# Dilated 3x3 convolution: an eight-row store on four DMA engines, moved from the last image pair to the first

## The chip, the cores and the metric

One core of one Trainium2 chip. The metric is the device time of one execution in microseconds. The figure for the kernel before is the median of six runs.

## The reference

The input x has 16 images of 64 channels, 64 x 64 pixels, in float32. The weights have 128 output channels, 64 input channels and 3 x 3 taps. The dilation is 2, so the input is padded by 2 on each side and the output has the same 64 x 64 pixels:

```python
for b, co, ci, kh, kw in ...:
    output[b, co] += weight[co, ci, kh, kw] * x_pad[b, ci, kh*2:kh*2+64, kw*2:kw*2+64]
```

The input is 16.8 MB, the output 33.6 MB, and each is moved once.

## The kernel before, in words

**Tiling.** Two images make a pair: their 2 x 64 input channels fill the 128 partitions, and a row of the partition is one channel of one image, 64 x 64 pixels. There are eight pairs (`npairs`). A pair is worked through in four groups (`NG`) of 16 output rows (`GR`), so the main loop over `G` (line 193) has 32 turns, with `pb` the pair and `g` the group in it.

**A turn.** ScalarE casts chunks of a pair's float32 tile `x32` to float16, several groups ahead (`casts`, line 153, which calls `cast`, line 68). VectorE adds pairs of rows (`rowsum`, line 77). TensorE makes three products in PSUM: psP from the row sums, psA and psB from the rows themselves (`product`, line 161); output rows come in blocks of four, of which two are psA + psP and two are psB + psP. ScalarE copies psP to SBUF (line 227), and VectorE does the two additions (line 234), which write the group's 16 rows of both images into the pair's output tile `osb`. That tile has 128 partitions, one for each output channel, and in each partition the first image's 64 rows and then the second's.

**Buffers.** `x32`, `x16` and `osb` have three buffers each. A load into an `x32` buffer waits until the casts of the pair three earlier have read it, and the additions into an `osb` buffer wait until the stores of the pair three earlier have landed.

**The order of the DMAs.** All loads and stores are issued from SyncE (SP) into one queue, in the order in which the program is written; SP stands still when an issue has to wait. The schedule is written by hand. Ahead of the loop come the weights (line 88), the first pair in two parts and the second and the third pair whole (lines 89 to 91; `load`, line 61, with the issue at line 64). The fourth pair's load is issued at the end of turn `G == 0` (lines 241 and 242), the fifth pair's at the end of the first pair (lines 253 and 254), later ones at the ends of pairs (line 243). A DMA also waits, eight DMAs later, for the one whose semaphore it takes over.

**Stores.** `store` (line 183) writes rows r0 to r1 of image m of a pair; its last argument cuts the 128 partitions into several DMAs, by default one. The middle pairs are stored at their end, 2 MB for each image (lines 255 to 257). The first and the last pair are stored in halves, after the second and the fourth group (lines 245 to 252), 1 MB for each image. One of these halves is cut further: for the second image of the last pair, rows 0 to 23 go out as one DMA (line 249) and rows 24 to 31 as two (line 250): 124 partitions (`FOUR`, line 190), and then the remaining 4, with 2 KB in each partition. `ROWS4` (line 191) is 8. The profile shows these two DMAs on four of the sixteen DMA engines.

**The end.** At line 290 SP waits for all stores to land, one semaphore after another.

Of the kernel before, what the change touches and what calls it, by code (L numbers as in the profile page):

```python
# [10 lines left out]
def kernel(  # L11
# [24 lines left out]
    GR = 16  # L36
# [24 lines left out]
    def load(pb, cuts=(0, H)):  # L61
        x32_tiles[pb] = fpool.tile([P, HW], f32, tag="x32", name="x32")
        for lo, hi in zip(cuts[:-1], cuts[1:]):
            nc.sync.dma_start(  # L64
                out=x32_tiles[pb][:, lo * W : hi * W], in_=x_pair[pb, :, lo * W : hi * W]
            )
# [10 lines left out]
    def rowsum(c):  # L77
        pb, g = divmod(c, NG)
        if g == 0:
            xs_tiles[pb] = sxpool.tile([P, HW // 2], f16, tag="xs", name="xs")  # L80
        v = x16_tiles[pb][:, g * GR * W : (g + 1) * GR * W].rearrange(
            "p (b e q) -> p b e q", e=2, q=2 * W
        )
        s = xs_tiles[pb][:, g * NH : (g + 1) * NH].rearrange("p (b q) -> p b q", q=2 * W)
        nc.vector.tensor_tensor(out=s, in0=v[:, :, 0], in1=v[:, :, 1], op=add)  # L85
# [67 lines left out]
    def casts(G):  # L153
        for n in range(2 if G else 3):
            c = ahead[0]
            if c >= ngroups or c > G + (7 if c < 2 * NG else 5):
                return
            cast(c)
            ahead[0] += 1

    def product(ps, src, kind, blk0, nblk, first, last):
        for j in (1, 0, 2):
            dw = (j - 1) * d
            o0, o1 = max(0, -dw), W - max(0, dw)
            t = kind * KW + j
            for hb in range(2):
                pp = slice(hb * CI, (hb + 1) * CI)
                rhs = src(pp, dw + o0, dw + o1)
                po = ps[:, hb * NH + blk0 * 2 * W : hb * NH + (blk0 + nblk) * 2 * W]
                po = po.rearrange("p (r w) -> p r w", w=W)[:, :, o0:o1]  # L170
                nc.tensor.matmul(  # L171
                    out=po,
                    lhsT=w_sb[pp, t * CO : (t + 1) * CO],
                    rhs=rhs,
                    start=first and j == 1,
                    stop=last and j == 2,
                )

    def blocks(x16, b0, n, e):
        v = x16.rearrange("p (b e r w) -> p b e r w", e=2, r=2, w=W)  # L180
        return lambda pp, c0, c1: v[pp, b0 : b0 + n, e, :, c0:c1]

    def store(pb, m, r0=0, r1=H, rows=((0, P),)):
        for lo, hi in rows:
            nc.sync.dma_start(
                out=out_img[2 * pb + m, lo:hi, r0 * W : r1 * W],
                in_=o_tiles[pb][lo:hi, m * HW + r0 * W : m * HW + r1 * W],
            )

    FOUR = ((0, P - 4), (P - 4, P))  # L190
    ROWS4 = 8

    for G in range(ngroups):
        pb, g = divmod(G, NG)
        x16 = x16_tiles[pb]
        xs = xs_tiles[pb].rearrange("p (r w) -> p r w", w=W)
        if g == 0:
            o_tiles[pb] = opool.tile([P, 2 * HW], f32, tag="osb", name="osb")
        o = o_tiles[pb].rearrange("p (m b e q) -> p m b e q", m=2, e=2, q=2 * W)
        b0 = g * NBLK  # L200

        def summed():
            ps = ppool.tile([P, 2 * NH], f32, tag="p", name="psP")
            sv = lambda pp, c0, c1: xs[pp, g * GR // 2 : (g + 1) * GR // 2, c0:c1]
            product(ps, sv, 0, 0, NBLK, True, True)
            return ps

        if G:
            psP = summed()

        psA = apool.tile([P, 2 * NH], f32, tag="ab", name="psA")
        product(psA, blocks(x16, b0, NBLK, 1), 1, 0, NBLK, True, False)
        z = 1 if g == 0 else 0
        product(psA, blocks(x16, b0 + z - 1, NBLK - z, 1), 2, z, NBLK - z, False, True)

        psB = apool.tile([P, 2 * NH], f32, tag="ab", name="psB")
        product(psB, blocks(x16, b0, NBLK, 0), 3, 0, NBLK, True, False)
        z = 1 if g == NG - 1 else 0
        product(psB, blocks(x16, b0 + 1, NBLK - z, 0), 4, 0, NBLK - z, False, True)

        if not G:
            psP = summed()

        if not G:
            casts(0)
        p_sb = spool.tile([P, 2 * NH], f32, tag="psb", name="p_sb")
        nc.scalar.copy(out=p_sb, in_=psP)  # L227
        if G:
            casts(G)
        if G + 1 < ngroups:  # L230
            rowsum(G + 1)
        pv = p_sb.rearrange("p (m b q) -> p m b q", m=2, q=2 * W)
        for e, ps in ((0, psA), (1, psB)):
            nc.vector.tensor_tensor(  # L234
                out=o[:, :, b0 : b0 + NBLK, e],
                in0=ps.rearrange("p (m b q) -> p m b q", m=2, q=2 * W),
                in1=pv,
                op=add,
            )

        if G == 0:
            load(XF)
        if g == NG - 1 and 0 < pb < npairs - XF - 1:
            load(pb + XF + 1)
        if pb in (0, npairs - 1):
            if g % 2 == 1:
                store(pb, 0, (g - 1) * GR, (g + 1) * GR)
                if pb and g == 1:
                    store(pb, 1, 0, 2 * GR - ROWS4)
                    store(pb, 1, 2 * GR - ROWS4, 2 * GR, FOUR)  # L250
                else:
                    store(pb, 1, (g - 1) * GR, (g + 1) * GR)
            if G == NG - 1:
                load(XF + 1)
        elif g == NG - 1:
            store(pb, 0)
            store(pb, 1)
# [37 lines left out]
```

## Time and profile before

| | |
|---|---|
| median of six runs | 126.95 us (126.77 to 127.29) |
| the profiled execution | 127.05 us |
| its span, first to last instruction | 125.2 us |
| DMA queue q1 | 50.63 MB, 96.5% of sixteen engines' span |
| busy: PE, DVE, ACT | 104.7, 91.0, 64.9 us |
| last store issued, last landing | 109.9 us, 124.34 us |

Times inside the execution are counted from the start of the span. The profile cuts the span into 40 slices; a digit is the busy share of a slice in tenths, and the row GB/s tells what the DMA engines moved in it. A DMA is cut into packets, which here are one partition's bytes each (16, 8, 6 or 2 KB), and the trace has the start and the duration of each packet, without the number of its engine. An engine takes its packets in order, back to back, so a chain of packets can often be followed. At the end of its share of a DMA an engine counts up a semaphore; this is a landing, and a DMA on sixteen engines has sixteen. Matmul ends are modelled.

### The profile page before, as it was taken

What the parts mean: (1) busy time and instruction counts of PE and PEld (TensorE: products, weight loads), DVE (VectorE), ACT (ScalarE), POOL (GpSimd) and SP (SyncE); (2) the same over time, 40 slices, a digit from 0 to 9 for tenths busy, and PEclk for the clock granted to TensorE, in tenths of its full rate; (3) what the DMA queues carried; (4) which work ended last, traced back from release to release, by engine and by line L of the source; (5) the groups of instructions that cost most, each with busy time, mean ns of one, the idle gap of its engine ahead of it and who ended that gap; (6) DMA issues with size and microseconds to landing.
All of it is one profiled execution on the core that took longest, in us unless ns stands there. A gap on an engine that the chain in (4) does not pass through costs nothing.

```text
span 125.2 us, 2339 instructions
## 1 busy us (share of the span) xinstructions
PE 104.7 (84%) x1000; PEld 56.3 (45%) x1000; DVE 91.0 (73%) x103; ACT 64.9 (52%) x68; POOL 2.2 (2%) x8
## 2 busy tenths in 40 slices
PE   6975999999999999999999999999999999500000
PEld 2342555555555555555555555555555555200000
DVE  0751998988898888988988898889888988700000
ACT  4368896665666566656665666566653333100000
POOL 2400000000000000000000000000000000000000
PEclk9999999999999999999999999999999999965555
DMA  4999999899999999999999999999999999999981
GB/s 133 383 452 445 419 414 429 275 419 416 453 448 419 414 435 429 427 435 419 429 435 421 429 435 429 419 429 435 435 419 429 429 429 429 429 414 414 429 374 71
DMA packets 4466, 50.78 MB, mean 406 GB/s; under 512 B 488, under 2 KB 488, under 8 KB 1000
## 3 DMA queue, kind: packets, MB, share of 16 engines
q1 hardware_dynamic: 4456, 50.63, 96.5%
q8 instruction: 8, 0.13, 0.4%
q14 instruction: 2, 0.02, 0.0%
HBM read 17.07 MB, written 33.55 MB: 404 GB/s over the span
## 4 chain that ended last, share of the span: by engine, by line
PE 76%; DMA 6%; ACT 2%; DVE 1%; DVEq 1%; SPq 1%; issue 0%
PE psA L171 31%; PE psB L171 30%; PE psP L171 16%; DMA x<-in_x_dram 6%; ACT x L73 2%; DVE osb L234 1%; DVEq L290 1%; ACT p_sb L227 1%; SPq L64 0%; SPq L88 0%; DVEq L234 0%
## 5 line engine op out<-in xcount | busy, mean ns | idle before, releaser
L171 PEld LDWEIGHTS <-w_sb 64*128 64x128 f16 x960 | 54.2, 94 | 47.1 <-issue 1.6
L227 ACT COPY p_sb<-psP 128x1024 f32<-128x1024 f32 x32 | 32.4, 1012 | 36.9 <-issue 21.6
L234 DVE TENSOR_TENSOR osb<-psA,p_sb 128x1024 f32<-128x1024 f32 x32 | 39.2, 1224 | 13.5 <-PE psA L171 9.5
L171 PE MATMUL psA<-x,w_sb 64*128 64x496 f16 (+3 forms) x384 | 45.1, 365 | 0.8 <-ACT x L146 0.8
L171 PE MATMUL psB<-x,w_sb 64*128 64x496 f16 (+3 forms) x384 | 45.1, 365 | 0.0
L234 DVE TENSOR_TENSOR osb<-psB,p_sb 128x1024 f32<-128x1024 f32 x32 | 39.1, 1221 | 0.0
L73 ACT CAST x<-x 128x1024 f16<-128x1024 f32 (+2 forms) x31 | 32.1, 1044 | 0.5 <-DMA x<-in_x_dram 0.5
L171 PE MATMUL psP<-xs,w_sb 64*128 64x496 f16 (+1 forms) x192 | 26.0, 371 | 1.3 <-ACT p_sb L227 1.3
L85 DVE TENSOR_TENSOR xs<-x 128x512 f16<-128x512 f16 x32 | 13.3, 416 | 0.7 <-ACT x L73 0.7
L101 PE MATMUL dm<-zero 128*128 128x512 f16 x10 | 4.1, 534 | 1.2 <-DVE zero L93 1.2
L111 DVE CAST wd<-w 128x192 f16<-128x192 f32 x1 | 0.5, 501 | 2.4 <-DMA w<-in_weight_dram 2.4
L101 PEld LDWEIGHTS <-zero 128*128 128x128 f16 x10 | 1.1, 124 | 2.6 <-issue 1.3
L124 PEld LDWEIGHTS <-wd 128*64 128x64 f16 x30 | 1.0, 118 | 1.7 <-DVE wd L111 1.1
L124 PE MATMUL wt<-ident,wd 128*64 128x128 f16 x30 | 1.6, 241 | 0.2 <-DVE wd L111 0.2
L113 ACT ACT_TABLE_LOAD x1 | 1.3, 1283 | 0.7 <-PEq L276 0.7
L113 ACT CAST wd<-w 128x192 f16<-128x192 f32 x1 | 0.5, 540 | 1.5 <-DMA w<-in_weight_dram 1.5
L136 ACT CAST w_sb<-wt 128x384 f16<-128x384 f32 x1 | 0.5, 478 | 1.4 <-PE wt L124 1.4
L146 ACT CAST x<-x 128x512 f16<-128x512 f32 x1 | 0.6, 617 | 0.9 <-DMA x<-in_x_dram 0.9
L143 DVE CAST x<-x 128x640 f16<-128x640 f32 x1 | 0.5, 493 | 0.6 <-DMA x<-in_x_dram 0.6
L93 DVE MEMSET zero<- 128x256 uint32 x1 | 0.3, 272 | 0.9 <-PEq L276 0.9
L138 DVE CAST w_sb<-wt 128x384 f16<-128x384 f32 x1 | 0.6, 557 | 0.5 <-PE wt L124 0.5
L112 POOL TENSOR_TENSOR wd<-w 128x192 f16<-128x192 f32 x1 | 0.8, 797 | 2.3 <-DMA w<-in_weight_dram 2.3
(11 smaller groups left out, 4.1 us busy)
## 6 DMA issues: line engine op xcount, KB each, us to landing
out_dram<-osb SPq DMA_DIRECT2D x12, 2048.0 KB, 18.9
x<-in_x_dram SPq DMA_DIRECT2D x7, 2048.0 KB, 17.1
out_dram<-osb SPq DMA_DIRECT2D x7, 1024.0 KB, 13.0
x<-in_x_dram SPq DMA_DIRECT2D x1, 1088.0 KB, 5.7
x<-in_x_dram SPq DMA_DIRECT2D x1, 960.0 KB, 7.5
out_dram<-osb SPq DMA_DIRECT2D x1, 768.0 KB, 15.7
w<-in_weight_dram SPq DMA_DIRECT2D x1, 288.0 KB, 2.8
out_dram<-osb SPq DMA_DIRECT2D x1, 248.0 KB
```

The source lines that it names most:

```text
L73: nc.scalar.copy(out=x16_tiles[pb][:, lo * W : hi * W], in_=x32_tiles[pb][:, lo * W : hi * W])
L85: nc.vector.tensor_tensor(out=s, in0=v[:, :, 0], in1=v[:, :, 1], op=add)
L101: nc.tensor.matmul(out=dm[:, 0:512], lhsT=zero[:, 0:P], rhs=zero)
L112: nc.gpsimd.tensor_tensor(out=wdv[:, 3], in0=wv[:, 0], in1=wv[:, 1], op=sub)
L113: nc.scalar.copy(out=wdv[:, 2], in_=wv[:, 0])
L124: nc.tensor.matmul(out=wts[k % 3][r * CI : (r + 1) * CI, c0 + j * CO : c0 + (j + 1) * CO], lhsT=wd[:, t * CI : (t + 1) * CI], rhs=ident,)
L138: nc.vector.tensor_copy(out=t2[0], in_=t2[1])
L146: nc.scalar.copy(out=x16_tiles[0][:, 0 : 8 * W], in_=x32_tiles[0][:, 0 : 8 * W])
L171: nc.tensor.matmul(out=po, lhsT=w_sb[pp, t * CO : (t + 1) * CO], rhs=rhs, start=first and j == 1, stop=last and j == 2,)
L227: nc.scalar.copy(out=p_sb, in_=psP)
L234: nc.vector.tensor_tensor(out=o[:, :, b0 : b0 + NBLK, e], in0=ps.rearrange("p (m b q) -> p m b q", m=2, q=2 * W), in1=pv, op=add,)
L290: with _tile.TileContext(nc) as tc:
```

## The change

The three DMAs for rows 0 to 31 of the last pair's second image become one. The eight rows that go to four engines are now rows 0 to 7 of the first image of the first pair. They are stored as 124 and then 4 partitions at the end of turn `G == 0`, the first turn, ahead of the issue of the fourth pair's load. The first pair's first half-image store begins at row 8 and has 24 rows. The number of DMAs is the same.

```diff
         if G == 0:
+            store(0, 0, 0, ROWS4, FOUR)
             load(XF)
...
         if pb in (0, npairs - 1):
             if g % 2 == 1:
-                store(pb, 0, (g - 1) * GR, (g + 1) * GR)
-                if pb and g == 1:
-                    store(pb, 1, 0, 2 * GR - ROWS4)
-                    store(pb, 1, 2 * GR - ROWS4, 2 * GR, FOUR)
-                else:
-                    store(pb, 1, (g - 1) * GR, (g + 1) * GR)
+                store(pb, 0, ROWS4 if G == 1 else (g - 1) * GR, (g + 1) * GR)
+                store(pb, 1, (g - 1) * GR, (g + 1) * GR)
```

On SP the order from the third pair's load on was: fourth load, four half-image stores, fifth load. It becomes: 124-partition store, 4-partition store, fourth load, 24-row store, three half-image stores, fifth load.

## Prediction

> **What bounds the kernel now.** I read the page's slices first, then the kernel's waits, then a table by stage, then the DMA queue's own order, and last the trace's records of single packets and landings. The page's slices:
>
> ```profile
> PE   6975999999999999999999999999999999500000
> DMA  4999999899999999999999999999999999999981
> GB/s 133 383 452 445 419 414 429 275 419 416 453 448 419 414 435 429 427 435 419 429 435 421 429 435 429 419 429 435 435 419 429 429 429 429 429 414 414 429 374 71
> q1 hardware_dynamic: 4456, 50.63, 96.5%
> ```
>
> A slice is 3.13 us. PE stops in slice 34 (109 us), the DMA engines go on to the end. Their one queue, q1, fills 96.5% of sixteen engines' span. Two things stand out in the rates: slice 7 (21.9 to 25.0 us) has 275 GB/s where its neighbours have 419 to 429, and the last slice has 71. SP's own waits say what ends the run:
>
> ```profile
> SPq L290 <- DMA out_dram<-osb: 13.4, 3, 8.8
> ```
>
> The closing wait (L290) stands 13.4 us for stores after the last one was issued. The page's chain of waits, which gives PE 76%, follows the last DVE instruction and doesn't pass through these stores; I don't use it for the end. The stage tables (window and its length, busy time and count by engine, clock, DMA share, GB/s):
>
> ```profile
> 12.00:18.00 6.00, 6.00 (x58) 3.23 (x59) 5.91 (x7) 4.99 (x6) 0.00 (x0) 1.00 1.02 431
> 20.50:24.00 3.50, 3.50 (x40) 2.04 (x38) 3.30 (x4) 2.55 (x3) 0.00 (x0) 1.00 0.97 288
> 30.00:60.00 30.00, 30.00 (x296) 16.50 (x292) 26.68 (x30) 18.64 (x20) 0.00 (x0) 1.00 1.01 431
> ...
> 120.00:121.00 1.00, 0.00 (x0) 0.00 (x0) 0.00 (x0) 0.00 (x0) 0.00 (x0) 0.50 0.91 385
> 121.00:122.00 1.00, 0.00 (x0) 0.00 (x0) 0.00 (x0) 0.00 (x0) 0.00 (x0) 0.50 0.78 328
> 122.00:123.00 1.00, 0.00 (x0) 0.00 (x0) 0.00 (x0) 0.00 (x0) 0.00 (x0) 0.50 0.39 164
> 123.00:124.00 1.00, 0.00 (x0) 0.00 (x0) 0.00 (x0) 0.00 (x0) 0.00 (x0) 0.50 0.16 66
> ```
>
> From 12 to 120 us the engines are always occupied, so each engine ends when its own sum of work is done. From 120 on they drop out one by one: the end is that of the slowest engine. Between 20.5 and 24 they are occupied (0.97) but move 288 GB/s instead of 431: something slows every packet there. SP's order around the change:
>
> ```profile
> 11.07 0.33 SPq L64 DMA_DIRECT2D x<-in_x_dram  x1
> 16.97 7.04 SPq L185 DMA_DIRECT2D out_dram<-osb  x4
> 24.11 6.54 SPq L64 DMA_DIRECT2D x<-in_x_dram  x2
> ...
> 60.03 50.51 SPq L185 DMA_DIRECT2D out_dram<-osb  x14
> ```
>
> The fourth pair's load goes out at 11.07, the first store at 16.97.
>
> **What the Trainium skill says.** "DMA: Bandwidth & Descriptors", section "Why a DMA increments its semaphore by 16 and not by 1": a DMA runs on the largest number of engines up to 16 that divides its slowest dimension, the lowest-numbered ones. So 124 partitions run on four engines, 31 each, and 4 partitions on the same four. The trace agrees: the 128 packets of 2 KB (115.7 to 119.1 us) form four back-to-back chains of 32, one every 80 ns, and of each of the two DMAs four landings of single engines are recorded. Section "Latency and other measured facts" there gives about 0.6 us to the first byte for this kind of issue; the trace's first DMA issues from 0.74 to 1.12 and its first packet starts at 1.76. Section "Two DMAs through the same engine are not ordered": descriptors start in order but are pipelined; so a store may begin to disturb before its recorded packets. No page that I read bears on the dip at 21 to 24 us.
>
> **The change part by part.**
>
> *What a store of eight rows costs, late or early.* On the low four engines 32 packets of 80 ns, 2.56 us each engine; on the twelve others nothing. In the store beside it, which shrinks from 32 rows to 24, every engine's eight packets fall from 309 to 234 ns, 8 x 75 = 0.60 us. So against an even store the low four carry +1.96 us and the others -0.60. Before, that sits in the last pair (6 KB packets at L249, 2 KB at L250); after, in the first pair. The same packets on the same engines: **each engine's sum of work is unchanged**, 0 us. There are 22 stores either way.
>
> *Which engine ends last.* The last landings of the last store are 123.33, 123.52, 123.80, 124.17, 124.23 and 124.34 us. The low four can be followed: their landings of the four-partition store at 118.72, 119.02, 119.46, 119.57, plus two shares of 8 KB stores at about 2.36 and 2.43, give 123.5, 123.8, 124.2, 124.3. So three of the last four are low engines, and 124.17 is another one, late since about 16 us (below). The span of 125.17 ends 0.83 after the last landing; the profiled execution is 127.05, so 1.88 lies around its span, and 127.05 is 0.10 above the runs' median of 126.95. I add differences to the median.
>
> *The fourth load waits on SP.* Its place in the queue is now behind two stores, which need the first group's two DVE additions. They end at 13.13 + 1.22 = 14.35. Two issues at 0.55 to 0.60 each (the spacings of these two stores now, 104.28, 104.88, 105.47) put the load at about 15.6 instead of 11.07. First packets about 1.0 us after the issue starts (0.74 to 1.76): 16.6. The third pair's load ends on its engines at 17.74 to 18.27 in fourteen cases, 18.55 and 19.40 in the others, so about 1.1 us of cover remains: cost 0. Without the cover, the twelve engines would idle for what the issue is late; they end, but for the late one, at 123.33 or earlier and have 1.0 us to spare, and the late one has 2.8 us of cover here. Behind the waiting store on SP stands only this load; then the stores of 16.97, which find SP free. Bound: 0 to +0.3.
>
> *Later landing of the fourth load.* The low four start it 2.56 us later: about 24.2 + 2.6 = 26.8, or 27.8 with the slowing below; the ACT cast that needs it runs at 32.52. Hidden, by 4.7 us. The fifth load's low shares move by 1.96, from 38.5 to 39.1 to at most 41.1, no later than its latest landing today (41.20), against a cast at 44.88. The output buffer's reuse is the tightest: DVE at 85.23 writes a tile whose store lands at 84.96; that is the late engine's landing, and the low four, 82.4 to 83.0 plus 2, stay at it or below. Even a stall of 1 us there is covered by the backlog: the last stores are issued at 109.5 and 109.9, and engines reach them at 116 to 119.
>
> *The dip.* It costs each engine most of a microsecond and happens once. The fourth load should take eight packets of 0.607, 4.86 us, and takes the fourteen punctual engines 5.73 from landing to landing (18.04 to 23.77): 0.87 lost. It begins at about 20.8 on packets 6 to 8 of the load, just ahead of the first stores, and no later change from loads to stores shows it (around 43.3 the excess is two packets, 0.7 us in all). So I take it for a cost of the first writes, by inference. An engine still **reading** when the others turn to writing loses more: the one that began this load at 18.55 lost 1.18, the one at 19.40 (held up by an instruction fetch of 0.92 at 16.15) lost 6.63 - 4.86 = 1.77, and its packets slow until 25. That is the engine that ends at 124.17.
>
> After the change the low four begin this load at 17.9 + 2.56 = 20.5, later than any engine now, and the twelve others turn to writing at about 22.9. If what slows readers is each engine's own first writes, the low four stand where the late engine stood: 1.8 to 1.9 lost instead of 0.87, +0.9 to +1.0; with only twelve of sixteen engines turning, 12/16 x 1.85 = 1.39, +0.52. I take +0.55, on engines that end last with nothing to hide it. If one first touch is paid for all, the low four pay it at 18 instead of 23: 0. If four writers make a smaller disturbance and leave nothing for the others, down to -0.87. So the bounds are -0.87 and +1.0. Sum: 0 + 0 + 0 + 0.55, **127.5 us**.
>
> **The rivals.** *Zero sum*: the same packets at another time, 126.95 (126.7 to 127.2). For it: engines occupied from 12 to 120, and a first touch that may be shared. Against: readers in the dip lose twice as much. *The dip dissolves*, the one on the faster side: the low four's early writes take the first-write cost when the other twelve aren't yet writing, so 0.87 vanishes on the low four and the late engine loses no more than before. Its place is 20.5 to 24 us, its price -0.87 at most, 126.1; it decides once the low four lose under 0.6 us there in all, and the late engine must gain too, since 124.17 is only 0.17 below the end. Half of it gives 126.5. Against: the low four are the ones that write first and would pay themselves. *Two dips*, one at 17 and one at 23, or the cover of the late load failing: +1.0 to +1.9, 128.0 to 128.9. That the change doesn't do what it says: the four chains of 2 KB packets exist today, and nothing in the early store differs but its time; small.
>
> **How the numbers follow.** Readers slowed, 127.5 (127.15 to 127.9): 0.40. Zero sum: 0.28. Dip dissolves, 126.1 to 126.7: 0.24. Two dips or a gap: 0.08. A measurement of this kernel can tell about 0.2%, 0.25 us. Slower by more: 0.36 of the first, all of the last, 0.44. Within: 0.04 of the first, 0.25 of zero sum and 0.01 of the third, 0.30. Faster: 0.23 and 0.03, 0.26. The range leaves out the lower part of the dissolved dip (below 126.2, about 0.08) and most of two dips (above 128.0, 0.08). Slower and faster cases share the chances, so: the likeliest case alone is 127.15 to 127.9.
>
> **What would show it.** In the profile after: 128 packets of 2 KB between about 17.7 and 21 us on four engines; the fourth load issued at 15.2 to 16; GB/s between 20.5 and 25; the fourth load's landings, with four at about 27.8 if readers are slowed, 26.8 if zero sum, and the others at 23.1 if the dip is gone; the last landings, whether four engines end at 124.9 or later. I am wrong if the dip is absent or elsewhere, if the twelve engines show a gap before the fourth load, or if engines other than these five end last.

## The result and the profile after

| | before | after |
|---|---|---|
| median, range, runs | 126.98 us (126.59 to 127.46, 38) | 127.80 us (127.06 to 129.31, 19) |
| ratio to before, 95% | | 1.0065 [1.0047, 1.0083] |
| the same kernel measured once more | 126.92 us (46 runs) | 127.42 us (6), 1.0039 [1.0017, 1.0061] |

The changed kernel is slower by half a microsecond to 0.8 us. The profile taken with the first series is of a run of 129.31 us in which TensorE began late, so all lines of "after" below are from the profile of the second measurement, an execution of 127.34 us with a span of 125.6 us (0.4 us more than before, a little less than either pair of medians shows). Every profile here is of one execution; the medians rest on several.

The rates in 40 slices, and the one queue:

```profile
GB/s 130 365 439 444 428 368 405 351 420 417 446 433 423 449 428 418 431 423 428 428 433 425 428 438 418 433 428 428 433 438 412 423 433 433 423 420 423 425 347 60
q1 hardware_dynamic: 4456, 50.63, 96.2%
```

The bytes and the packets of q1 are those of before. Slice 7 has 351 GB/s where it had 275, so the dip at 22 to 25 us is shallower; but slice 5 (15.7 to 18.8 us), at 414 before, now has 368. One dip has become two. The end is thicker: slice 38 has 347 (374 before). The queue on SP around the change:

```profile
14.41 0.70 SPq L185 DMA_DIRECT2D out_dram<-osb  x2
15.24 0.37 SPq L64 DMA_DIRECT2D x<-in_x_dram  x1
17.00 7.22 SPq L185 DMA_DIRECT2D out_dram<-osb  x4
24.32 6.37 SPq L64 DMA_DIRECT2D x<-in_x_dram  x2
```

The two early stores go out at 14.41, the fourth load at 15.24 (11.07 before), and the four half-image stores at 17.00, 0.03 later than before. In the last pair the first store is issued at 103.27, before at 103.23: the computation has lost nothing. The stage table, with the columns as in the prediction (window and its length, busy time and count by engine, clock, DMA share, GB/s):

```profile
16.00:18.00 2.00, 2.00 (x24) 1.04 (x20) 1.91 (x3) 2.00 (x4) 0.00 (x0) 1.00 1.01 385
18.00:20.50 2.50, 2.50 (x26) 1.32 (x24) 2.16 (x3) 2.07 (x4) 0.00 (x0) 1.00 1.02 402
20.50:24.00 3.50, 3.50 (x39) 2.03 (x37) 3.26 (x4) 2.66 (x3) 0.00 (x0) 1.00 0.95 333
30.00:60.00 30.00, 30.00 (x296) 16.38 (x294) 26.76 (x30) 18.64 (x20) 0.00 (x0) 1.00 1.01 431
...
121.00:122.00 1.00, 0.00 (x0) 0.00 (x0) 0.00 (x0) 0.00 (x0) 0.00 (x0) 0.50 0.76 320
122.00:123.00 1.00, 0.00 (x0) 0.00 (x0) 0.00 (x0) 0.00 (x0) 0.00 (x0) 0.50 0.37 156
123.00:124.00 1.00, 0.00 (x0) 0.00 (x0) 0.00 (x0) 0.00 (x0) 0.00 (x0) 0.50 0.23 98
124.00:125.00 1.00, 0.00 (x0) 0.00 (x0) 0.00 (x0) 0.00 (x0) 0.00 (x0) 0.50 0.02 8
```

Up to 60 us the DMA share stays at 0.95 to 1.02: nothing there shows an engine that starves. Between 16 and 18 us the engines are as busy as elsewhere but move 385 GB/s; the kernel before moves 442 there:

```profile
16.00:18.00 2.00, 2.00 (x22) 1.09 (x20) 1.91 (x3) 2.00 (x4) 0.00 (x0) 1.00 1.06 442
```

From 30 to 60 us the rate is 431 in both. At the end, 123 to 124 us has a DMA share of 0.23 where it was 0.16, and there is something left after 124. SP's closing wait agrees; it is longer than the 13.4 us of before by 0.7:

```profile
SPq L287 <- DMA out_dram<-osb: 14.1, 5, 4.5
```

The landings of the four low engines, from the trace's landing records (before: the ones that the prediction followed):

```
                        before                          after
third load              18.04 to 18.61 (14 of 16)       18.92  19.16  19.31  19.42
4-partition store       118.72 119.02 119.46 119.57     21.61  21.82  21.98  22.09
fourth load             about 24.2                      26.90  27.01  27.24  27.34
last store              123.5  123.8  124.2  124.3      124.19 124.28 124.52 124.73
```

(For the third load after, the four are those that fit the starts of the four chains of 2 KB packets, 18.60 to 19.1 us.)

The mean landing of the last store over all sixteen engines is 122.79, before 122.69. So the engines together have lost 0.1 us, the four low ones 0.5 (means 123.95 and 124.43), and they end last: the next engine lands at 123.74. Another count says the same. I added what each packet of 16 KB took beyond 0.611 us, from 14 to 28 us, for all engines, leaving out packets beside an instruction fetch (a 16 KB packet of another queue): 16.7 us before, all of it after 20.3 us; 14.7 us after, of which 4.5 lie before 20.3 us. The slowing in all has not grown. More of it falls on the four engines that had no reserve.

### The profile page after: what moved, and what is told of

Its sections match the earlier page's. It is cut to its first block, busy times and chain, and to the rows that moved or that the text cites. A ratio compares the mean times of both kernels' runs of the same rounds, so it can differ in the third digit from the quotient of the medians.

```text
span 127.5 us, 2340 instructions
## 1 busy us (share of the span) xinstructions
PE 107.1 (84%) x1000; PEld 56.4 (44%) x1000; DVE 90.8 (71%) x103; ACT 65.0 (51%) x68; POOL 2.3 (2%) x8
## 4 chain that ended last, share of the span: by engine, by line
PE 81%; DMA 2%; DVE 1%; DVEq 1%; ACT 1%; issue 0%
PE psA L171 32%; PE psB L171 30%; PE psP L171 16%; DMA w<-in_weight_dram 2%; PE wt L124 2%; PE dm L101 2%; DVE osb L234 1%; DVEq L287 1%; ACT p_sb L227 1%; DVE wd L111 0%; DVEq L234 0%
## 5 line engine op out<-in xcount | busy, mean ns | idle before, releaser
L171 PE MATMUL psA<-x,w_sb 64*128 64x496 f16 (+3 forms) x384 | 46.0, 371 | 0.0
L101 PE MATMUL dm<-zero 128*128 128x512 f16 x10 | 5.0, 623 | 1.2 <-DVE zero L93 1.2
L124 PEld LDWEIGHTS <-wd 128*64 128x64 f16 x30 | 1.5, 162 | 2.6 <-DVE wd L111 1.3
L124 PE MATMUL wt<-ident,wd 128*64 128x128 f16 x30 | 2.2, 314 | 0.4 <-DVE wd L111 0.4
L138 DVE CAST w_sb<-wt 128x384 f16<-128x384 f32 x1 | 0.6, 558 | 1.2 <-PE wt L124 1.2
L148 DVE CAST w_sb<-wt 128x384 f16<-128x384 f32 x1 | 0.6, 558 | 0.4 <-PE wt L124 0.4
L115 POOL CAST wd<-w 128x192 f16<-128x192 f32 x1 | 0.8, 815 | 0.0
## 6 DMA issues: line engine op xcount, KB each, us to landing
out_dram<-osb SPq DMA_DIRECT2D x12, 2048.0 KB, 20.3
```

What stands on the lines that cost most here:

```text
L101: nc.tensor.matmul(out=dm[:, 0:512], lhsT=zero[:, 0:P], rhs=zero)
L115: nc.gpsimd.tensor_copy(out=wdv[:, 4], in_=wv[:, 2])
L124: nc.tensor.matmul(out=wts[k % 3][r * CI : (r + 1) * CI, c0 + j * CO : c0 + (j + 1) * CO], lhsT=wd[:, t * CI : (t + 1) * CI], rhs=ident,)
L138: nc.vector.tensor_copy(out=t2[0], in_=t2[1])
L171: nc.tensor.matmul(out=po, lhsT=w_sb[pp, t * CO : (t + 1) * CO], rhs=rhs, start=first and j == 1, stop=last and j == 2,)
```

## The experiments

Four theories stood against each other. **Slowed readers**: the four low engines fall 2.56 us behind while loads still follow, are then reading when the other twelve have turned to writing, and lose more than those. **An early dip**: what the early store adds is a second slow stretch by its first writes. **The late load**: the issue of the fourth load at 15.24 instead of 11.07 costs something after all. **The end**: it is not the early store that costs, but that the last pair is no longer cut.

### The eight rows behind the load, and the late load alone

The first kernel has all of the change, but the fourth load goes ahead of the two stores (the diff is against the changed kernel):

```diff
         if G == 0:
+            load(XF)
             store(0, 0, 0, ROWS4, FOUR)
-            load(XF)
```

> The eight-row store on four engines stays in the first turn but is issued behind the fourth pair's load, so that load goes out at about 11 us again. Slowed readers (four engines that start the fourth load 2.56 us late read on while the twelve others turn to writing and lose about 1 us more): gone, since all sixteen read that load together: 127.0 us. Late load (the issue waits for the first group's additions and comes too close to when the engines need it, so that its first packets take 1.0 to 1.2 us instead of 0.61): gone too, 127.0. If the place of the eight rows in the run matters by itself, 127.8 as with the change.

127.69 us, 1.0068 [1.0041, 1.0096]: the load is issued at 11.20, as before, and the whole price is still there. The stage table around the turns from loads to stores:

```profile
16.00:18.00 2.00, 2.00 (x22) 1.07 (x20) 1.91 (x3) 2.00 (x3) 0.00 (x0) 1.00 1.04 434
...
20.50:24.00 3.50, 3.50 (x40) 2.04 (x36) 3.17 (x4) 2.60 (x3) 0.00 (x0) 1.00 0.95 303
...
43.00:45.00 2.00, 2.00 (x22) 1.11 (x20) 1.99 (x3) 0.89 (x1) 0.00 (x0) 1.00 0.90 360
```

There is no dip at 16 to 18 us, the one at 20.5 stands about as before, and a new one stands at 43 to 45 us (360 GB/s), at the next turn from loads to stores. The kernel before has 401 there:

```profile
43.00:45.00 2.00, 2.00 (x23) 1.03 (x19) 1.85 (x3) 1.02 (x2) 0.00 (x0) 1.00 0.95 401
```

So neither the early dip nor the late load is needed for the loss. Slowed readers, as I had put the theory, missed as well: all sixteen engines read the fourth load together here, and it asked for 127.0. I widened it to any later load that the four read late; the kernels with later pairs below are the test of that.

The second kernel is the one before with nothing changed but the time of that load. A copy of 128 elements on VectorE, behind the first group's additions, reads one column of the buffer that the load will fill:

```diff
         if G == 0:
+            late = wpool.tile([P, 1], f32, name="late")
+            nc.vector.tensor_copy(out=late, in_=x32_tiles[0][:, 0:1])
             load(XF)
```

> The kernel before, with one added VectorE copy of a 128 x 1 column of the first input tile behind the first group's additions, so that the fourth pair's load has to wait for it as it does with the change; no early store. Late load: about 127.8, as with the change, and packets of over 0.9 us where the load begins, near 18 us. Slowed readers: 127.0, one dip at 21 to 24 us.

126.99 us, 0.9995 [0.9971, 1.0018]. The trace has the load at 14.57. The late load alone costs nothing that shows, so it has fallen as a cause.

### The early store on sixteen engines

The kernel before, with the first eight rows stored early on all sixteen engines; the last pair stays cut:

```diff
         if G == 0:
+            store(0, 0, 0, ROWS4)
             load(XF)
...
-                store(pb, 0, (g - 1) * GR, (g + 1) * GR)
+                store(pb, 0, ROWS4 if G == 1 else (g - 1) * GR, (g + 1) * GR)
```

> The kernel before, with its cut store in the last pair, and rows 0 to 7 of the first image stored early by all sixteen engines, ahead of the fourth load, which waits as with the change. Slowed readers: no engine is late, so about 127.0 (the finer packets add 8 x 9 ns = 0.07); the dip comes once, at 17 to 19 us, if it belongs to the first writes, and at 21 to 24 if it doesn't. Late load: less than with the change, since all engines have 0.64 us of store packets as cover: 127.0 to 127.5. Two dips on all engines: 127.9.

127.04 us, 1.0013 [0.9992, 1.0033]. Its stage table:

```profile
16.00:18.00 2.00, 2.00 (x22) 1.10 (x20) 1.91 (x3) 2.00 (x4) 0.00 (x0) 1.00 1.06 377
...
20.50:24.00 3.50, 3.50 (x40) 2.06 (x38) 3.29 (x4) 2.55 (x3) 0.00 (x0) 1.00 0.95 385
```

The early dip is here too, as deep as after the change (377 and 385 GB/s), and the later one is nearly gone (385; 288 before). Lengthened packets sum to 8.2 us from 14 to 28 us (16.7 before), and the mean last landing is 122.38, 0.31 earlier. The median doesn't gain: in the profiled run a single engine lands last at 124.73, 0.77 behind the next. An early dip, shared evenly, costs nothing that shows here.

### The eight rows issued from ScalarE

The fourth load first on SP; the eight rows issued on ScalarE's own queue at the end of turn `G == 1` (`store` takes the issuing engine as one more argument); the rest as in the change, against which the diff stands:

```diff
         if G == 0:
-            store(0, 0, 0, ROWS4, FOUR)
             load(XF)
+        if G == 1:
+            store(0, 0, 0, ROWS4, FOUR, nc.scalar)
```

> The fourth load goes out at 11 us as in the kernel before, and the eight-row store on four engines is issued from ScalarE's queue at the end of the second turn, at about 16 us, so that its packets mix with the loads'. Slowed readers: the four engines are late in the fourth load all the same: 127.5 to 128.0, four late landings of that load. Late load: nothing is late, 127.0.

127.35 us, 1.0029 [1.0013, 1.0045]. Slower than before, by less than in one queue. What an engine does with two queues was not followed, so this says only that another queue doesn't take the whole price away.

### The eight rows in later pairs

The last pair uncut, nothing early, and the cut moved to the first image of a middle pair N; four kernels, N = 1, 2, 3 and 5:

```diff
...
         elif g == NG - 1:
-            store(pb, 0)
+            if pb == N:
+                store(pb, 0, 0, ROWS4, FOUR)
+                store(pb, 0, ROWS4, H)
+            else:
+                store(pb, 0)
             store(pb, 1)
```

The queue has three more turns from loads to stores after the one at 22 us: at about 44, 58 and 73 us, the last behind the eighth pair's load. Four low engines that are late from pair 1 on meet two of these, from pair 2 on one, from pair 3 on none. Pair 1:

> The eight rows on four engines are those of the second pair's first image, issued at about 35 us, with two loads still to come behind them; the last and the first pair are stored whole. Lateness costs where engines still read when others turn to writing: two such turns remain, 127.1 to 127.6. A cost of the first writes alone: 127.0. A price of being late for long, whatever the traffic: about three quarters of the loss, 127.5.

127.71 us, 1.0063 [1.0030, 1.0095]. Pair 5:

> The same with the sixth pair, issued at about 85 us, when all loads have landed. Slowed readers in either form: no load follows, so zero sum holds, 127.0. A price of being late for long: some 25 of 106 us of lateness are left, 127.1 to 127.2; a price of any place but the last pair: 127.5 or more.

126.89 us, 1.0005 [0.9988, 1.0023]. Pairs 2 and 3, for the edge:

> The eight rows on four engines are the third pair's, issued at about 48 us; one load, the eighth pair's, still follows them in the queue. Slowed readers at a turn from loads to stores: some 4 to 12 us of lengthened packets in all near 70 to 75 us and 127.2 to 127.7. If only the first writes matter, or if a late place is harmless: 127.0.

127.77 us, 1.0068 [1.0045, 1.0090]. Pairs 1 and 2 lie just above the ranges given for slowed readers, and one turn costs no less than two.

> The same with the fourth pair, issued at about 60 us, directly behind the last load in the queue. Slowed readers: no load follows, no lengthened packets, 127.0, though the place is only 12 us later than in the run beside it. A price of being late for long: 127.3 or more.

127.01 us, 1.0001 [0.9977, 1.0026]. The edge is sharp: one load behind the eight rows, and the price is paid in full; none behind them, and there is none. The theory that it costs when the last pair is no longer cut falls with pairs 3 and 5, where it is uncut too and no price is paid. The stage tables at the turns, first of pair 1:

```profile
56.00:58.00 2.00, 2.00 (x22) 1.09 (x20) 1.58 (x3) 1.79 (x2) 0.00 (x0) 1.00 1.09 369
58.00:60.00 2.00, 2.00 (x26) 1.23 (x22) 2.00 (x3) 1.05 (x2) 0.00 (x0) 1.00 0.86 319
72.00:74.00 2.00, 2.00 (x24) 1.18 (x22) 1.84 (x4) 1.55 (x2) 0.00 (x0) 1.00 0.98 418
```

of pair 2:

```profile
58.00:60.00 2.00, 2.00 (x24) 1.18 (x22) 1.58 (x3) 1.87 (x2) 0.00 (x0) 1.00 1.01 420
...
72.00:74.00 2.00, 2.00 (x25) 1.23 (x22) 2.00 (x3) 1.05 (x2) 0.00 (x0) 1.00 0.96 352
```

and of pair 3:

```profile
58.00:60.00 2.00, 2.00 (x26) 1.18 (x23) 2.00 (x3) 1.05 (x2) 0.00 (x0) 1.00 1.00 426
...
72.00:74.00 2.00, 2.00 (x24) 1.17 (x22) 1.84 (x4) 1.58 (x2) 0.00 (x0) 1.00 1.00 422
```

The kernel before has no dip in either place:

```profile
58.00:60.00 2.00, 2.00 (x24) 1.22 (x22) 2.00 (x3) 1.05 (x2) 0.00 (x0) 1.00 1.06 451
...
72.00:74.00 2.00, 2.00 (x24) 1.14 (x21) 1.84 (x3) 1.69 (x2) 0.00 (x0) 1.00 1.02 434
```

The dip comes at the next turn once four engines are late: with pair 1 it stands at the turn at 58 us (319 GB/s), with pair 2 at the one at 73 us (352), with pair 3 nowhere after the first turn. With pair 1 the load that ends at 58 to 62 us takes the five latest engines, which include the four, 5.8 to 6.4 us from landing to landing (55.10, 55.18, 55.27, 55.48, 56.07 to 61.20, 61.26, 61.59, 61.83, 61.88), the sixteen on average 5.66, and where nothing slows it 4.85. Its six last landings are 124.41 to 125.18, and those of pair 3 end at 124.36, like before.

It is not the four alone that lose here. With pair 2 the load behind the cut takes the sixteen engines 5.33 us on average, where the same load takes 4.84 with pair 3, and the four latest, 5.27 to 5.42, don't stand out. The mean of the last landings is 123.32 with pair 1 and 123.27 with pair 2, 0.6 above the 122.69 of before (122.65 with pair 3), so the slowing in all has grown. Nor do engines stand idle for it: the time of all packets, divided by sixteen, grows by as much, from 121.35 us before to 122.03 and 121.87.

### A very small early store, and an even one ahead of the four

The kernel before, with only 4 partitions of the eight rows stored early, one packet on each low engine. The other 124 follow behind the load, as 112 and 12 partitions. The last pair stays cut:

```diff
         if G == 0:
+            store(0, 0, 0, 8, ((P - 4, P),))
             load(XF)
...
+                if G == 1:
+                    store(0, 0, 0, 8, ((0, 112), (112, P - 4)))
-                store(pb, 0, (g - 1) * GR, (g + 1) * GR)
+                store(pb, 0, 8 if G == 1 else (g - 1) * GR, (g + 1) * GR)
```

> The kernel before, with its cut store in the last pair; ahead of the fourth load, only 4 partitions of rows 0 to 7 are stored, one 2 KB packet on each of four engines, which makes nobody late. If the early first writes of four engines cost by themselves: lengthened packets at 16 to 19 us beside those at 21 to 24, 127.2 to 127.5. If it takes the lateness: 127.0.

127.33 us, 1.0040 [1.0012, 1.0068]. The stage table and the closing wait:

```profile
16.00:18.00 2.00, 2.00 (x22) 1.03 (x19) 1.91 (x3) 2.00 (x4) 0.00 (x0) 1.00 1.04 437
...
20.50:24.00 3.50, 3.50 (x39) 2.04 (x36) 3.33 (x4) 2.55 (x3) 0.00 (x0) 1.00 0.92 260
```

```profile
SPq L293 <- DMA out_dram<-osb: 14.0, 1, 14.0
```

By the time alone this run lies in the range of the rival, first writes that cost by themselves (127.2 to 127.5), and not at the 127.0 of lateness. The trace has none of the dip that this rival asks for: there is no early one (437 GB/s), and the later one is as deep as ever. Four packets of 2 KB neither bring the first nor spare the second. The last landing is at 124.42, 0.08 later than before. Most of the rest comes after it: the span of 125.5 ends 1.07 us behind the last landing, before 0.83. This kernel has three more stores, and one closing wait of 14.0 us stands where there were three; that the other waits then follow one by one after the last landing is my reading of the 0.24 us, not shown. (The three kernels here with one more store end 0.93 us behind theirs.) Without it, 0.2% remains, which the interval doesn't tell from none.

The changed kernel with eight rows of the second image stored on sixteen engines, ahead of the four engines' store:

```diff
         if G == 0:
+            store(0, 1, 0, 8)
             store(0, 0, 0, ROWS4, FOUR)
             load(XF)
...
-                store(pb, 1, (g - 1) * GR, (g + 1) * GR)
+                store(pb, 1, 8 if G == 1 else (g - 1) * GR, (g + 1) * GR)
```

> The changed kernel, with eight rows of the second image stored by all sixteen engines ahead of the eight rows on four. If the four engines lose because they make the first writes alone: these are shared now, 127.0 to 127.2. If they lose because they are late in the loads that follow: 127.4 to 127.8, as with the change.

127.68 us, 1.0060 [1.0037, 1.0083]. The even store doesn't take the price away. The trace, of an execution of 128.80 us, shows where it goes: this time the fourth load takes the four low engines 4.77 to 4.96 us (landings 22.27, 22.30, 22.40, 23.74 to 27.17, 27.26, 27.30, 28.51), as if nothing slowed it. At the turn at 44 us it is their turn all the same:

```
                    before the load            after it                   taken
nine earliest       37.83 to 38.13             42.70 to 43.02             4.84 to 4.88
three between       38.16  39.02  39.49        44.34  44.56  44.61        6.18  5.53  5.11
four low engines    40.64  40.72  40.76  41.97 46.32  46.41  46.53  48.18 5.68  5.69  5.77  6.20
```

(Landings are paired in their order; of the three between, an instruction fetch of 0.97 us at 42.61 falls on one.) The nine earliest lose nothing there, the four readers 0.8 to 1.3 us. This is the barest view of slowed readers that I have, and it is from one execution.

### A version that might have gained

The even early store had shortened the dip, so I gave the four engines six rows in the last pair instead of eight:

```diff
-    ROWS4 = 8
+    ROWS4 = 6
...
+            store(0, 0, 0, 8)
             load(XF)
...
-                store(pb, 0, (g - 1) * GR, (g + 1) * GR)
+                store(pb, 0, 8 if G == 1 else (g - 1) * GR, (g + 1) * GR)
```

> The early eight rows on all sixteen engines as in the run before of that kind, whose mean last landing lay 0.31 us below that of the kernel before while four engines ended last; with six instead of eight rows on the four engines in the last pair, so that these have 0.64 us less and every other engine 0.16 more. If only these four set the end there: 126.4 to 126.6. If the late engine beside them does: 127.0.

127.06 us, 1.0021 [1.0002, 1.0039]. It beats neither the kernel before nor the even store with eight rows. In the profiled run fifteen engines land by 123.65 and one at 125.10: the balance among fifteen was better, and in that execution one late engine decided. No version beat the kernel before.

## Why the prediction was right, and where it was not

**The time.** 127.5 was forecast, 127.8 and 127.4 were measured. The sign, the size and the engines that pay are those of the forecast.

**Each engine's work is unchanged: right.** With the eight rows in pair 3 or 5 the time is that of before (1.0001, 1.0005). The place costs nothing by itself, as long as no load follows.

**Which engines end last: right.** The four low ones, by 0.45 us.

**The load that waits on SP, and its later landing: 0, right.** The load issued late alone gave 0.9995, and the last pair's first store goes out 0.04 us later.

**The dip: the right size from the wrong parts, and so in part luck.** I had put +0.52 on the fourth load of the low four and rounded it to 0.55: they would still be reading it when the twelve others turn to writing, and lose 1.39 us there instead of 0.87. They lost 0.39 (5.19 to 5.29 us from landing to landing, where 4.86 is unslowed), and the twelve others about 0.86 (5.7 us). So in the changed kernel the late readers lost less in the second dip than the others, not more; their landings, 26.90 to 27.34, lie nearer to the 26.8 that stood for zero sum than to the 27.8 for slowed readers. What made up for it was not in the sum: the dip at 16 to 18 us. It caught the four on their last packets of the third load, ahead of their own early store, and they landed that load at about 18.9 to 19.4 us (19.2 on average), where before fourteen of sixteen had landed it by 18.61 (18.3 on average). The nearest of the branches in the prediction is the one in which the four pay at 18 us instead of 23, and which it priced at 0: they lost about 0.9 there, and the 0.39 on top. Against the 0.87 of before this makes +0.3 to +0.4 at the landing of the fourth load (27.12 on average against 26.8), and +0.5 at the end. The early dip was in the rival of two dips, at a price of 1.0 to 1.9 and a chance of 0.08. It came, but the second dip became shallower by as much as the first took.

The inference behind the step, "So I take it for a cost of the first writes", failed too: in four kernels a slow stretch comes again, at 44 us (the eight rows behind the load, and behind an even store), at 58 (pair 1) and at 73 (pair 2). I had looked for it at later turns in the kernel before, where those four engines are not late, and where it could not be seen.

**The zero sum** holds for the sixteen engines together (mean landing +0.10), not for the four. **The dissolved dip** needed the twelve to land the fourth load at 23.1; they landed it from 23.98 on.

| the eight rows in | loads to stores, turns still ahead | ratio |
|---|---|---|
| pair 0, ahead of the fourth load (the change) | 4 | 1.0065, 1.0039 |
| the change with an even store ahead | 4 | 1.0060 |
| pair 0, behind the fourth load | 3 | 1.0068 |
| pair 1 | 2 | 1.0063 |
| pair 2 | 1 | 1.0068 |
| pair 3, pair 5 | 0 | 1.0001, 1.0005 |

The price is paid about once, however many turns remain. What the medians show is its condition: it comes when a load still follows on the engines that the eight rows have made late, and doesn't come when none follows. How it is paid differs from kernel to kernel. In the changed kernel the four lose it ahead of their own early store, and at 44 us, though late, they are not slowed (4.85 us for that load). With the even store ahead the four lose it at 44 us, while the nine earliest lose nothing; with pair 1 most engines lose, and the four among the most; with pair 2 all lose about alike. So slowed readers is seen as such in one trace, and is not shown to be the mechanism in all of these kernels.

Open, then, are why it isn't paid at each turn, and what in the memory or the engines slows a read near a turn to writing. A kernel without any uneven store was not run, so what the cut itself costs isn't known. Nor was one in which no engine reads while others write, with all loads ahead of all stores: three buffers don't hold the eight pairs.

## What to carry to other kernels

In this kernel, where one queue fills all DMA engines, moving an uneven store was not free, although each engine's sum of work stayed the same: it cost 0.4 to 0.7% where a load still followed on the engines that it made late, and nothing that shows where none did. So the first place to try for such a store is behind the last load. Before calling a slow stretch a cost of the first time, ask what was special in that place, and make that happen again elsewhere. And look at the mean of the last landings beside the last one: a change can leave the first as it is and move the second by half a microsecond.

## What the runs showed of the hardware

- Reads slow down well ahead of the first packet of the store that follows them: in the kernel before the first lengthened read of the dip is at 20.77 us and the first store packet starts at 23.43, in the changed kernel 15.93 and 18.60, with the even store 15.42 and 18.10. The Trainium skill ("DMA: Bandwidth & Descriptors", section "Two DMAs through the same engine are not ordered") has descriptors pipelined, with read and write sides apart; the trace agrees in so far as the reads slow down before the store's own records begin, but no run here shows what slows them.
- A 16 KB read that takes 0.61 us takes up to 1.3 us in such a stretch in the changed kernel (at 22.45 us), and up to 1.9 us in the kernel before (at 22.95 us).
- The span ends 0.83 us after the last landing in the kernels with 22 stores, 0.93 in the three with 23 and 1.07 in the one with 25.
